# When a convolution block squares its input tiles: four early in order, four later, instead of eight in pairs

## The chip, the cores and the metric

The kernel runs on one core of a Trainium2 chip. The core has five engines that run their own instruction lists in order: TensorE (PE in the profile; PEld is its weight load), VectorE (DVE), ScalarE (ACT), GpSimd (POOL) and SyncE (SP). They meet only at semaphores, and each transfer (DMA) raises one when it has landed. The metric is the device time of one execution in microseconds (us); before the change it is 2095.65 us (median of three runs, 2095.22 to 2095.98).

## The reference

The program is a two-layer trunk on x of 1024 positions by 1024 channels, all in float32. Cut to the part that matters here, layer 0 starts so:

```python
def rms_norm(x, g):
    y = xf * lax.rsqrt(jnp.mean(xf * xf, axis=-1, keepdims=True) + EPS)
    return y * g

def short_conv_mixer(h, w_in, conv_k, w_out):
    b, c, u = jnp.split(h @ w_in, 3, axis=-1)
    y = causal_depthwise_conv(c * u, conv_k)      # width 3
    return (b * y) @ w_out

x = x + short_conv_mixer(rms_norm(x, mix_norm[0]), ...)   # layer 0
x = x + swiglu(rms_norm(x, ffn_norm[0]), ...)
# layer 1: dilated attention and a second swiglu, then a last rms_norm
```

The norm's scale per position needs the sum over all 1024 channels of the squares of x.

## The kernel before

**Tiles.** x is held transposed, as eight tiles X[0] to X[7] of 128 channels by 1024 positions. The gain is multiplied into the operands at once; the factor per position (`rstd`) is applied to the products' results, so that TensorE can start before the squares are summed.

**The products.** The projection by `conv_w_in` is done by Strassen's scheme in Winograd's form: twelve units u, each of seven products m. One product is twelve matmuls (`Strassen.mm`, L586 to L588): for each of four tiles k the high half of the weights with the high and the low half of the operand, then the low half of the weights with the high half of the operand. High and low halves carry a float32 number in two pieces. The first products, counted from 0, are (u,m) = (0,1) (1,1) (0,2) (1,2) (2,1) (2,2) (3,1) (3,2) (4,1) (4,2) (0,6) (1,6) (0,7) (1,7) (0,5) (1,5) (0,4) (1,4) (2,6) (0,3).

**What feeds them.** `load_raw` (L171, SP) loads a slab of weights, `raw`, of 512 KB. `combo` (L208, DVE) adds or subtracts such slabs. `split` makes the two halves `w` of the weights: ACT the high one (L147), DVE the low one (L148). The operand tiles `b` of the left side come from X by `operand` (L896 on ACT, L897 on DVE), or from sums `t2`, `t3` of X tiles by `hi` (L578 on ACT, L579 on DVE). `save` (L592, ACT) and `add` (L596, DVE) take results out of the PSUM banks.

**What sets the order.** Nothing is scheduled: instructions stand on each engine as the Python text issues them. `Conv.mix` has a function `start(n)` that runs before the matmuls of product n+1 are issued, that is, after product n. It makes operands (`next(prep)`), makes weights ahead (`ensure`), and calls `squares`. `mm` itself makes the weights two products ahead (three from n = 20 on), and when the next key needs a `combo`, that is made before.

**The squares.** `squares(n)` squares X[n] on ACT over all 1024 columns. X[0] and X[4] are squared straight into two sums, `norm.acc` and `self.upper` (L907). The other six go to a page `sq` (L910), and POOL issues a DMA of 512 KB that adds the page to its sum (L911). Two additions into the same sum may not be in flight at once, so the second waits until the first has landed; additions into the two sums may overlap. After product 18 DVE adds `upper` to `acc` (L1112).

**Pages.** Tiles of 128 by 1024 float32 come from one pool of 41 pages. A page is given out again when its last reader is known; whoever writes it next waits for that reader. A `sq` page is read by its adding DMA, so the next writer of that page waits until this DMA has landed.

Of the kernel before, what the change touches and what calls it, by code (L numbers as in the profile page):

```python
# [103 lines left out]
def trunk(ctx: ExitStack, tc: tile.TileContext, x, gains_in, cwi, ck, cwo, wqkv, wo, relb,  # L104
# [73 lines left out]
    def ensure(upto):  # L178
        while op_state[0] < min(upto + 1, len(ops)):
            key = ops[op_state[0] + 1][0] if op_state[0] + 1 < len(ops) else None  # L180
            if key in sums_of:
                sums_of.pop(key)()
            made[op_state[0]] = ops[op_state[0]][1]()
            op_state[0] += 1
# [208 lines left out]
    def run(*gens):  # L393
        for _ in zip(*gens):
            pass
        for g in gens:
            for _ in g:
                pass
# [485 lines left out]
    class Conv(Strassen):  # L884
# [182 lines left out]
        def mix(self, group1):  # L1067
            norm = self.norm
            prep = self.operands()
            stats = norm.stats(0, S)  # L1070

            def start(n):
                if n == 0:
                    next(prep)
                    ensure(self.at(2, 2))
                elif n in (1, 2):
                    next(prep)
                elif n == 3:
                    self.first(0)
                    ensure(self.at(4, 1))  # L1080
                    self.squares(0, 4)
                elif n == 4:
                    self.first(1)
                    ensure(self.at(4, 2))
                    self.squares(1)
                elif n == 5:
                    ensure(self.at(0, 6))
                    self.squares(5)
                elif n == 6:
                    ensure(self.at(1, 6))  # L1090
                    self.squares(2)
                elif n == 7:
                    next(prep)
                    self.squares(6, 3)
                elif n == 8:
                    self.first(2)
                    ensure(self.at(0, 7))
                    self.squares(7)
                elif n == 9:
                    next(prep)  # L1100
                    next(prep)
                elif n in (10, 12):
                    next(prep)
                elif n == 11:
                    next(prep)
                    self.first(3)
                elif n == 13:
                    self.first(4)
                elif n == 14:
                    next(prep, None)  # L1110
                elif n == 18:
                    nc.vector.tensor_tensor(out=norm.acc, in0=norm.acc, in1=self.upper, op=ALU.add)  # L1112
                    del self.upper
                elif n == 20:
                    self.ahead = 3

            def gather():
                next(stats)
                next(stats)

            def spread():
                run(stats)
                nc.scalar.activation(norm.acc, norm.rstd, AF.Square)
                self.ready = True

            self.base = op_state[1]
            ensure(self.at(0, 1))
            next(prep)
            ensure(self.at(0, 2))
            self.run(start, {(0, 3): gather, (2, 5): spread})  # L1130
            group1("co", self.plain, self.hid)

# [937 lines left out]
```

## Time and profile before

| what | value |
|---|---|
| median of three runs | 2095.65 us |
| lowest, highest | 2095.22, 2095.98 us |
| the profiled execution, its own time | 2097.12 us |
| its span in the profile | 2095.3 us |
| PE busy | 2077.0 us, 99% |
| DVE busy | 1756.8 us, 84% |
| ACT busy | 1023.0 us, 49% |
| POOL busy | 246.7 us, 12% |
| granted TensorE clock over the span | 0.998 |

In rows of the timeline stand the start, the duration, engine, line, operation, output and input, the count, and in brackets the idle time of the engine ahead of it with what ended it. Several equal instructions in a row are merged into one row (x4); its duration is then from the first start to the last end. DMA rows of SP and POOL are the issue of a transfer; it lands some us later. In rows of stretches (A:B) stand the length, busy time and count per engine, the granted TensorE clock, the busy share of the 16 DMA engines and the GB/s.

### The profile page before, as it was taken

What the parts mean: (1) busy time and instruction counts of PE and PEld (TensorE: products, weight loads), DVE (VectorE), ACT (ScalarE), POOL (GpSimd) and SP (SyncE); (2) the same over time, 40 slices, a digit from 0 to 9 for tenths busy, and PEclk for the clock granted to TensorE, in tenths of its full rate; (3) what the DMA queues carried; (4) which work ended last, traced back from release to release, by engine and by line L of the source; (5) the groups of instructions that cost most, each with busy time, mean ns of one, the idle gap of its engine ahead of it and who ended that gap; (6) DMA issues with size and microseconds to landing.
All of it is one profiled execution on the core that took longest, in us unless ns stands there. A gap on an engine that the chain in (4) does not pass through costs nothing.

```text
span 2095.3 us, 30793 instructions
## 1 busy us (share of the span) xinstructions
PE 2077.0 (99%) x10978; PEld 1790.3 (85%) x10978; DVE 1756.8 (84%) x3308; ACT 1023.0 (49%) x1892; POOL 246.7 (12%) x352
## 2 busy tenths in 40 slices
PE   9999999999999999999999999999999999999998
PEld 7788888888888888888789999998788888888887
DVE  8798759988888888968985888987998888888886
ACT  8333427444443455446544666665544434456433
POOL 1000000110100010010223333311011001001000
PEclk9999999999999999999999999999999999999999
DMA  7322643233333467451656867855223333359432
GB/s 221 96 96 71 227 135 81 101 106 109 103 106 103 139 209 214 130 169 61 228 194 196 214 166 228 235 185 146 71 90 107 106 101 112 109 196 246 159 96 81
DMA packets 124729, 300.72 MB, mean 144 GB/s; under 512 B 15084, under 2 KB 37694, under 8 KB 124576
## 3 DMA queue, kind: packets, MB, share of 16 engines
q1 hardware_dynamic: 90720, 201.94, 32.0%
q0 software_dynamic: 26224, 82.11, 12.6%
q10 hardware_dynamic: 7632, 14.70, 1.9%
q8 instruction: 87, 1.43, 0.3%
q14 instruction: 66, 0.54, 0.1%
HBM read 208.42 MB, written 82.93 MB: 139 GB/s over the span
## 4 chain that ended last, share of the span: by engine, by line
PE 91%; DVE 4%; ACT 1%; issue 1%; DMA 0%; DVEq 0%; SPq 0%; ACTq 0%
PE bank L588 20%; PE bank L586 20%; PE bank L587 20%; PE bank L1667 5%; PE bank L390 4%; PE bank L388 4%; PE bank L389 4%; PE bank L681 3%; PE bank L680 3%; PE bank L678 3%; PE bank L1536 2%; PE bank L1538 1%; PE bank L1537 1%; PE bank L1593 1%; PE bank L1592 1%; DVE b L579 1%
## 5 line engine op out<-in xcount | busy, mean ns | idle before, releaser
L588 PE MATMUL bank<-b,w 128*128 128x512 f32 x2008 | 782.9, 390 | 4.1 <-DVE w L148 3.9
L586 PE MATMUL bank<-b,w 128*128 128x512 f32 x2008 | 782.9, 390 | 3.1 <-ACT w L147 1.6
L587 PE MATMUL bank<-b,w 128*128 128x512 f32 x2008 | 782.6, 390 | 0.6 <-DVE b L897 0.6
L588 PEld LDWEIGHTS bank<-b,w 128*128 128x128 f32 x2008 | 377.4, 188 | 85.9 <-DVE w L148 7.6
L586 PEld LDWEIGHTS bank<-b,w 128*128 128x128 f32 x2008 | 377.6, 188 | 81.1 <-ACT w L147 3.5
L587 PEld LDWEIGHTS bank<-b,w 128*128 128x128 f32 x2008 | 377.6, 188 | 77.8 <-DVE b L897 1.4
L147 ACT ACTIVATE w<-combo 128x512 fp32r<-128x512 f32 (+2 forms) x496 | 254.2, 542 | 238.8 <-DVE combo L208 221.9
L148 DVE TENSOR_TENSOR w<-combo,w 128x512 fp32r<-128x512 f32 (+2 forms) x496 | 281.8, 581 | 40.6 <-ACT w L147 39.9
L592 ACT ACTIVATE part<-bank 128x512 f32<-128x512 f32 x192 | 114.4, 596 | 394.9 <-PE bank L588 392.4
L148 DVE TENSOR_TENSOR w<-raw,w 128x512 fp32r<-128x512 f32 (+2 forms) x348 | 192.5, 574 | 34.1 <-ACT w L147 34.1
L596 DVE TENSOR_TENSOR part<-part,bank 128x256 f32<-128x256 f32 (+1 forms) x372 | 174.8, 498 | 35.8 <-PE bank L588 18.8
L147 ACT ACTIVATE w<-raw 128x512 fp32r<-128x512 f32 (+2 forms) x348 | 170.7, 532 | 46.2 <-PE bank L588 12.2
L388 PE MATMUL bank<-w_hi,w 128*128 128x512 f32 (+1 forms) x400 | 151.3, 378 | 0.1
L390 PE MATMUL bank<-w_hi,w 128*128 128x512 f32 (+1 forms) x400 | 149.3, 373 | 0.7 <-DVE w L148 0.7
L389 PE MATMUL bank<-w_lo,w 128*128 128x512 f32 (+1 forms) x400 | 149.1, 373 | 0.0
L816 DVE TENSOR_TENSOR x<-x,bank 128x512 f32<-128x512 f32 x136 | 92.5, 680 | 28.0 <-PE bank L588 28.0
L208 DVE TENSOR_TENSOR combo<-raw 128x512 f32<-128x512 f32 (+1 forms) x176 | 113.8, 647 | 0.0
L507 DVE TENSOR_TENSOR x<-x,bank 128x512 f32<-128x512 f32 (+1 forms) x104 | 66.6, 643 | 54.0 <-PE bank L390 52.9
L390 PEld LDWEIGHTS bank<-w_hi,w 128*128 128x128 f32 x400 | 75.3, 188 | 15.0 <-DVE w L148 1.6
L388 PEld LDWEIGHTS bank<-w_hi,w 128*128 128x128 f32 x400 | 75.5, 189 | 12.0 <-ACT w L147 0.5
L389 PEld LDWEIGHTS bank<-w_lo,w 128*128 128x128 f32 x400 | 75.5, 189 | 11.6
L579 DVE TENSOR_TENSOR b<-hin,b 128x512 fp32r<-128x512 f32 x126 | 79.5, 684 | 6.0 <-ACT b L578 6.0
(228 smaller groups left out, 3342.1 us busy)
## 6 DMA issues: line engine op xcount, KB each, us to landing
hin<-part SPq DMA_DIRECT2D x126, 256.0 KB, 4.5
raw<-in_ffn_w_gate SPq DMA_DIRECT2D x44, 512.0 KB
raw<-in_ffn_w_up SPq DMA_DIRECT2D x44, 512.0 KB, 3.8
part<-sum POOLq DMA_DIRECT2D x72, 256.0 KB, 2.3
raw<-in_ffn_w_down SPq DMA_DIRECT2D x48, 384.0 KB, 3.7
raw<-in_attn_w_qkv SPq DMA_DIRECT2D x27, 512.0 KB, 3.7
raw<-in_conv_w_in SPq DMA_DIRECT2D x24, 512.0 KB, 3.6
part<-part POOLq DMA_DIRECT2D x36, 256.0 KB, 2.5
```

The lines of the kernel that those rows point to most:

```text
L147: nc.scalar.activation(hi, src, AF.Copy)
L148: low = lambda: eng.tensor_tensor(out=lo, in0=src, in1=hi, op=ALU.subtract)
L208: eng.tensor_tensor(out=c, in0=a, in1=b, op=op)
L388: nc.tensor.matmul(b, whi[:, a], ahi[:, s], start=first, stop=False)
L389: nc.tensor.matmul(b, whi[:, a], alo[:, s], start=False, stop=False)
L390: nc.tensor.matmul(b, wlo[:, a], ahi[:, s], start=False, stop=last)
L586: nc.tensor.matmul(b, hi[:, a], bhi, start=start and k == 0, stop=False, skip_group_check=True)
L587: nc.tensor.matmul(b, hi[:, a], blo, start=False, stop=False, skip_group_check=True)
L588: nc.tensor.matmul(b, lo[:, a], bhi, start=False, stop=k == n - 1, skip_group_check=True)
L592: nc.scalar.activation(t, b, AF.Copy)
L596: nc.vector.tensor_tensor(out=t, in0=t, in1=b, op=ALU.add)
L1667: nc.tensor.matmul(view(acc[ih], off, dims), vx[:, u * 192 + 128 * a:u * 192 + 128 * a + 128], rhs, start=first, stop=last)
```

## The change

`squares` is called with one tile at a time and at other places: X[0], X[1], X[2], X[3] after products 3, 4, 5, 6, and X[4], X[5], X[6], X[7] after products 9, 10, 11, 12. Before it was X[0] and X[4] after product 3, X[1] after 4, X[5] after 5, X[2] after 6, X[6] and X[3] after 7, X[7] after 8. The call also moves from the end of `start(n)` to its beginning, ahead of `next(prep)`, `first` and `ensure`. `squares` itself is the same.

```diff
             stats = norm.stats(0, S)
+            early = {3: 0, 4: 1, 5: 2, 6: 3, 9: 4, 10: 5, 11: 6, 12: 7}
 
             def start(n):
+                if n in early:
+                    self.squares(early[n])
                 if n == 0:
...
                 elif n == 3:
                     self.first(0)
                     ensure(self.at(4, 1))
-                    self.squares(0, 4)
                 elif n == 4:
                     self.first(1)
                     ensure(self.at(4, 2))
-                    self.squares(1)
                 elif n == 5:
                     ensure(self.at(0, 6))
-                    self.squares(5)
                 elif n == 6:
                     ensure(self.at(1, 6))
-                    self.squares(2)
                 elif n == 7:
                     next(prep)
-                    self.squares(6, 3)
                 elif n == 8:
                     self.first(2)
                     ensure(self.at(0, 7))
-                    self.squares(7)
```

Past the first 110 us or so of the span, the two programs differ only in which page a tile lies in. Names in the lists that follow: `x_99` to `x_106` are X[0] to X[7], `acc` and `acc2` the two sums, DMASW1 to DMASW6 the semaphores of the adding DMAs in their order, DMAHW those of SP's loads.

The adding DMAs on POOL, before:

```order
L911 DMA acc_374<-sq_402 128x1024 [waits Activation_49]
L911 DMA acc2_376<-sq_425 128x1024 [waits Activation_49]
L911 DMA acc_374<-sq_448 128x1024 [waits DMASW1_49,Activation_49]
L911 DMA acc2_376<-sq_476 128x1024 [waits DMASW2_49,Activation_49]
L911 DMA acc_374<-sq_479 128x1024 [waits DMASW3_49,Activation_49]
L911 DMA acc2_376<-sq_503 128x1024 [waits DMASW4_49,Activation_49]
```

and after the change:

```order
L911 DMA acc_364<-sq_393 128x1024 [waits Activation_49]
L911 DMA acc_364<-sq_417 128x1024 [waits DMASW1_49,Activation_49]
L911 DMA acc_364<-sq_442 128x1024 [waits DMASW2_49,Activation_49]
L911 DMA acc2_366<-sq_534 128x1024 [waits DMAHW7_49,DVE_49,Activation_49]
L911 DMA acc2_366<-sq_560 128x1024 [waits DMASW4_49,Activation_49]
L911 DMA acc2_366<-sq_585 128x1024 [waits DMASW5_49,Activation_49]
```

Before, the additions alternated between the sums and each waited for the one before the last; now three go into one sum and three into the other, and each waits for the one just ahead of it (the fourth, the first into the other sum, for its square alone).

ScalarE where product 6 gets its weights and the squares begin, before:

```order
L578 ACTIVATE b_347<-t2_313 128x512 [waits DVE_49]
L147 ACTIVATE w_365<-raw_111 128x512 [waits DMAHW7_49]
L147 ACTIVATE w_368<-raw_111 128x512
L147 ACTIVATE w_371<-raw_112 128x512 [waits DMAHW1_49]
L907 ACTIVATE acc_374<-x_99 128x1024
L907 ACTIVATE acc2_376<-x_103 128x1024 [waits DMAHW0_49]
L592 ACTIVATE part_392<-bank_379 128x512 [waits PE_49]
```

and after:

```order
L578 ACTIVATE b_347<-t2_313 128x512 [waits DVE_49]
L907 ACTIVATE acc_364<-x_99 128x1024
L147 ACTIVATE w_369<-raw_111 128x512 [waits DMAHW7_49]
L147 ACTIVATE w_372<-raw_111 128x512
L147 ACTIVATE w_375<-raw_112 128x512 [waits DMAHW1_49]
L592 ACTIVATE part_391<-bank_378 128x512 [waits PE_49]
```

The square of X[0] now stands ahead of the three weight halves, and that of X[4] has left this place.

ScalarE where the operands of m = 3 are made (`b_637` to `b_646`), ahead of the weights of product 17, before:

```order
L147 ACTIVATE w_621<-raw_108 128x512 [waits DMAHW0_49,Activation_49]
L896 ACTIVATE b_637<-x_103,gains_68 128x512 [waits Activation_49]
L896 ACTIVATE b_640<-x_104,gains_68 128x512
L896 ACTIVATE b_643<-x_105,gains_68 128x512 [waits Activation_49]
L896 ACTIVATE b_646<-x_106,gains_68 128x512 [waits DVE_49,PE_49]
L147 ACTIVATE w_656<-raw_113 128x512 [waits DMAHW2_49,DVE_49,PE_49]
```

and after:

```order
L147 ACTIVATE w_621<-raw_108 128x512 [waits DMAHW0_49]
L896 ACTIVATE b_637<-x_103,gains_68 128x512 [waits Activation_49]
L896 ACTIVATE b_640<-x_104,gains_68 128x512 [waits DMASW5_49,Activation_49]
L896 ACTIVATE b_643<-x_105,gains_68 128x512 [waits DVE_49,PE_49]
L896 ACTIVATE b_646<-x_106,gains_68 128x512 [waits DMASW6_49,Activation_49]
L147 ACTIVATE w_656<-raw_113 128x512 [waits DMAHW2_49,DVE_49,PE_49]
```

The second and the fourth of these operands now go to the pages of the squares of X[6] and X[7], and so wait for the fifth and the sixth adding DMA. On SP the first load after the start (`raw_619`) waited for the sixth adding DMA before and waits for the fourth now.

## The prediction

> **What bounds the kernel now.** I read the page first, then TensorE's waits up to 260 us, then the timelines of the engines there.
>
> ```profile
> span 2095.3 us, 30793 instructions
> PE 2077.0 (99%) x10978; PEld 1790.3 (85%) x10978; DVE 1756.8 (84%) x3308; ACT 1023.0 (49%) x1892; POOL 246.7 (12%) x352
> PE bank L588 <- DVE w L148: 2.7, 2, 2.0
> PE bank L586 <- ACT w L147: 1.6, 1, 1.6
> ```
>
> TensorE bounds the kernel, and the change touches no matmul. Only TensorE's idle time can move, and it can move only where the squares stand, in the first 65 us. Two stalls lie there: 1.6 us before product 6, for the high half of its weights, and 2.0 us inside product 17, for a low half.
>
> ```profile
> 25.13 0.50 PE L586 MATMUL bank<-b,w 128*128 128x512 f32 x1 [1.58 <-ACT w L147]
> 26.54 0.50 PE L588 MATMUL bank<-b,w 128*128 128x512 f32 x1 [0.67 <-DVE w L148]
> 57.02 0.39 PE L587 MATMUL bank<-b,w 128*128 128x512 f32 x1
> 59.43 0.80 PE L588 MATMUL bank<-b,w 128*128 128x512 f32 x1 [2.03 <-DVE w L148]
> 23.55:25.13 1.58, 0.00 (x0) 0.00 (x1) 1.48 (x3) 1.20 (x3) 0.00 (x0) 1.00 0.04 13
> 57.40:59.43 2.03, 0.00 (x1) 0.00 (x0) 1.35 (x3) 0.56 (x1) 0.00 (x0) 1.00 0.38 147
> 59.43:62.94 3.51, 3.51 (x9) 2.80 (x9) 3.51 (x7) 1.33 (x3) 0.00 (x0) 0.51 0.52 149
> 62.94:66.45 3.51, 3.51 (x17) 2.91 (x16) 1.78 (x3) 0.13 (x1) 0.00 (x0) 1.00 0.00 0
> ```
>
> The second stall costs more than its length: the granted clock was 0.51 in the 3.5 us behind it, and 9 matmuls started there against 17 in the next equal stretch. At half clock that is about 1.6 us lost. The first stall, 1.58 us, was followed by no lower clock, so 2.03 us is not far over what the gate lets pass.
>
> Why product 17 waits stands on VectorE.
>
> ```profile
> 52.13 0.68 DVE L148 TENSOR_TENSOR w<-raw,w 128x512 fp32r<-128x512 f32 x1
> 53.33 2.73 DVE L897 SCALAR_TENSOR_TENSOR b<-x,gains,b 128x512 fp32r<-128x512 f32 x4
> 55.98 0.68 DVE L208 TENSOR_TENSOR combo<-raw 128x512 f32<-128x512 f32 x1
> 58.08 0.69 DVE L208 TENSOR_TENSOR combo<-combo,raw 128x512 f32<-128x512 f32 x1 [1.42 <-DMA raw<-in_conv_w_in]
> 58.69 0.68 DVE L148 TENSOR_TENSOR w<-raw,w 128x512 fp32r<-128x512 f32 x1
> ```
>
> Its low half (58.69, done 59.37) stands behind four operands (L897) and two combinations of weights; the second of these waited for a slab. The slabs on SP:
>
> ```profile
> SPq L171 <- DMA acc<-sq: 32.2, 1, 32.2
> 49.07 0.33 SPq L171 DMA_DIRECT2D raw<-in_conv_w_in  x1
> 52.84 0.33 SPq L171 DMA_DIRECT2D raw<-in_conv_w_in  x1
> 54.76 0.33 SPq L171 DMA_DIRECT2D raw<-in_conv_w_in  x1
> ```
>
> SP sat 32 us on the last adding DMA before the first of these. The late slab is the second one; its issue at 52.84 follows the low half at 52.13, which frees its page (52.13 + 0.68 = 52.81), not the first slab.
>
> **The change, part by part.**
>
> *Product 6.* The square of X[0] now stands ahead of the three weight halves.
>
> ```profile
> 24.46 1.65 ACT L147 ACTIVATE w<-raw 128x512 fp32r<-128x512 f32 x3
> 25.80 1.89 DVE L148 TENSOR_TENSOR w<-raw,w 128x512 fp32r<-128x512 f32 x3
> 28.92 1.05 ACT L910 ACTIVATE sq<-x 128x1024 f32<-128x1024 f32 x1
> ```
>
> A square holds ScalarE for about 0.95 us (1.05, less the overlap with the next). The first weight half moves from 24.46 to 25.41, is ready at 26.04, and TensorE starts product 6 near 26.1. The low half can start at 26.1 instead of 25.80, so the third matmul moves only from 26.54 to about 26.85. TensorE is 0.3 us late from there. That lateness costs nothing, since it is idle at 57.40 anyway and what ends that wait is not in this chain: 0.
>
> *ScalarE from 26 to 50 us.* The eight squares are the same work. VectorE gets to the in-place subtraction about 1.2 us sooner, since four squares no longer stand ahead of the operands that it needs, and gives this back when the square of X[5] holds up the operands behind it. I put the low half of 52.13 at 51.9, and with it the second slab's issue at 52.6: a gain of 0.2 us at most if nothing else changes.
>
> *The chain of adding DMAs.* This is the term that counts.
>
> ```profile
> 30.28 0.88 POOL L911 DMA_DIRECT2D acc<-sq  x1 [28.30 <-ACT sq L910]
> 35.35 0.85 POOL L911 DMA_DIRECT2D acc<-sq  x1 [2.75 <-ACT b L578]
> 41.01 0.58 ACT L592 ACTIVATE part<-bank 128x512 f32<-128x512 f32 x1
> 43.83 0.86 POOL L911 DMA_DIRECT2D acc<-sq  x1 [1.98 <-ACT part L592]
> DMA to landing us min/median/max: 4.5/5.1/5.9
> ```
>
> The third DMA (35.35) waited for the first (30.28) to land: 5.07 us from issue to issue, 4.5 of it to landing. With two sums there were two under way, and POOL issued six from 30.28 to 43.83, one every 2.7 us. With one sum at a time each link takes 5.07. The square of X[1] runs 1.45 us sooner than at 28.92, since X[4]'s square (0.95) and a weight half (0.5) no longer stand ahead of it; so X[1], X[2], X[3] go out near 28.8, 33.9, 38.9 and disturb nobody. The square of X[5] stands on ScalarE behind the eviction that ran at 41.01; that one waits for product 10, whose end lets it run near 40.3, so the square is done near 41.9 and its DMA goes out at 42.2 (the 0.3 us of 28.92 + 1.05 to 30.28). It lands near 46.7. SP's first slab now waits for this one and goes out at 46.9, 2.2 us sooner than 49.07. Then X[6] goes out at 47.25 and X[7] only when X[6] has landed.
>
> These last two run beside slabs. Adding DMAs of the same size (512 KB) beside slabs are seen much later, in the down products of the feed-forward parts (`x` += `spill`, L831, groups of four). The landing of the first of each group, each from an answer of its own:
>
> ```profile
> DMA to landing us min/median/max: 5.6/5.6/5.6
> ...
> DMA to landing us min/median/max: 7.1/7.1/7.1
> ...
> DMA to landing us min/median/max: 7.4/7.4/7.4
> ...
> DMA to landing us min/median/max: 6.0/6.0/6.0
> ```
>
> With one slab ahead of it X[6] takes the least of these, 5.6: it lands at 52.9. X[7] goes out at 53.4, beside the slabs issued near 52.6 and 54.5; I take 6.1, so it lands at 59.5. Bounds: bare links (4.5 each) give 56.8; 5.9, the slowest of the first row, and then 7.1 give 60.8.
>
> *Who waits for X[7].* Its page goes to the last of the four operands of m = 3.
>
> ```profile
> 51.42 0.72 ACT L896 ACTIVATE b<-x,gains 128x512 fp32r<-128x512 f32 x1
> 54.27 0.63 ACT L147 ACTIVATE w<-raw 128x512 fp32r<-128x512 f32 x1 [2.12 <-PE bank L588]
> ```
>
> Nobody needs that operand before product 19. But ScalarE, which came to it at 51.42 and comes near 52.3 now, stops there, with the high half of product 17 (54.27) behind it; VectorE stops at the same operand (the fourth of 53.33), with both combinations and the low half behind it. From the landing: L896 0.7, L897 0.7, two combinations 0.7 and 0.6, the low half 0.7, 0.1 to TensorE: 3.5 us. Product 17 resumes at 59.5 + 3.5 = 63.0 instead of 59.43: +3.6 (bounds +0.9 and +4.9). The wait hides only if X[7] lands before 55.9. TensorE, VectorE and ScalarE move by the same amount behind it, so nothing is won back. The addition of the two sums (L1112) and the statistics stand behind products 18 and 19 and move along.
>
> *The clock.* The stall is now surely long enough for the lower clock. In the profiled execution it was paid already; that execution took 2097.12, 1.47 above the median, about what the lower clock costs. I take it that some executions did not pay it before, and that all do now: +0.8, half of 1.6. Bounds: -0.8, if half the slow stretch falls into the stall itself, and +1.7, if a second one follows.
>
> *Sum.* Against the profiled execution, which had paid the lower clock, 2097.12 + 3.6 = 2100.7. Against the median, 2095.65 + 3.6 + 0.8 = 2100.05. I forecast 2100.1.
>
> *A rule against it.* "DMA: Bandwidth & Descriptors" of the Trainium skill (section "Anatomy of one DMA — SWDGE (gpsimd) path") gives a DMA from GpSimd 2.0 us and its bytes over 436 GB/s: an estimate of 3.2 us for 512 KB. By it X[7] would land at 52.9 and the sum would be 0. The trace's 4.5 us, without a neighbour, disagrees, and the measurement decides.
>
> **The rivals.**
>
> *The wait on X[7] does not bind* (not slower). From 42.2 the chain has 13.7 us until 55.9; that needs links of 4.2 us, landing and reissue. The rule above would give it. Then the second slab alone sets product 17, at 59.2 (-0.2): 2095.4. If that slab also comes without its delay, VectorE's 1.42 us of waiting and the lower clock go too: 2095.65 - 1.4 - 1.6 = 2092.7, still within 0.2%. Against it: no DMA of line 911 landed under 4.5.
>
> *Bare links.* The slabs are through before the adding DMAs begin, and X[7] lands at 56.8: +0.9, and +0.3 for the clock: 2096.9. Against it: all four rows beside slabs are over 5.5.
>
> *The start decides.* The 0.95 us ahead of product 6 grows the first stall from 1.58 to 2.5 us, more than what brought the lower clock at 59.43. A slow stretch at 25 us would cost up to 1.6 us, but it would end in the idle time of product 17, like the 0.3 us above; 2100.1 stays.
>
> **How the numbers follow.** 0.2%, about what a measurement of this kernel can tell from no change, is 4.2 us: up to 2099.8. The wait on X[7] beside slabs has 0.85; its spread (landing 58.0 to 60.8, clock -0.8 to +1.7) gives 2097.5 to 2102.2, of which I put 0.57 above the bound and 0.28 below. Bare links have 0.08, the unbinding wait 0.07, nearly all within the bound (0.02 for a gain over 4.2 us that no row explains). So slower 0.57, same 0.28 + 0.08 + 0.05 = 0.41, faster 0.02. The range from 2096.9 to 2102.2 leaves the unbinding wait and the tails out.
>
> **What would show it.** In the profile after: ScalarE idle near 53 to 59 us in front of an L896, ended by the DMA of acc2; VectorE idle in front of its fourth L897; POOL's last three DMAs more than 5 us apart, the last issued after 53; SP's first slab near 47; TensorE idle first for a high half (L147), then for a low half (L148), together near 6 us between 56.5 and 63, and a clock near 0.5 behind. Wrong if the last adding DMA lands before 56, if TensorE resumes by 60, or if a stall appears outside the first 70 us.

## The result

The changed kernel takes 2103.19 us (median of 6 runs, 2102.71 to 2104.65), the kernel before beside it 2095.43 us (2094.52 to 2096.23, 6 runs). The ratio is 1.0037, with an interval from 1.0027 to 1.0048: 7.8 us slower. The forecast was 2100.1 with a range from 2096.9 to 2102.2, so the sign was right and the size was too small. The profiled execution took 2103.45 us.

The page after:

```profile
span 2101.7 us, 30794 instructions
PE 2079.5 (99%) x10978; PEld 1792.1 (85%) x10978; DVE 1757.8 (84%) x3308; ACT 1023.9 (49%) x1892; POOL 246.7 (12%) x352
```

What TensorE waits for in the first 260 us (us in total, times, the longest):

```profile
PE bank L586 <- ACT w L147: 7.8, 2, 5.3
PE bank L588 <- DVE w L148: 1.0, 1, 1.0
```

The work is the same. The waits for a high half (L147) have grown from 1.6 us to 7.8 us; one of the two is 5.3 us long. TensorE's timeline shows where:

```profile
26.05 0.50 PE L586 MATMUL bank<-b,w 128*128 128x512 f32 x1 [2.56 <-ACT w L147]
63.55 0.79 PE L586 MATMUL bank<-b,w 128*128 128x512 f32 x1 [5.26 <-ACT w L147]
65.75 0.79 PE L588 MATMUL bank<-b,w 128*128 128x512 f32 x1 [0.98 <-DVE w L148]
```

Product 6 starts at 26.05, 0.92 us later than before. Product 17 waits 5.26 us for its first high half and 0.98 us for the low half, and is through at 65.75, where it was at 59.43. These 6.32 us are nearly the whole difference of the two profiled executions (2103.45 - 2097.12 = 6.33). The rest of the 7.8 us is that the execution profiled before was a dear one, 1.69 us above the median of 2095.43, and the one profiled after only 0.26 above its own.

ScalarE and VectorE in front of product 17, after:

```profile
55.20 1.34 ACT L896 ACTIVATE b<-x,gains 128x512 fp32r<-128x512 f32 x2 [2.07 <-DMA acc<-sq]
62.26 0.72 ACT L896 ACTIVATE b<-x,gains 128x512 fp32r<-128x512 f32 x1 [5.72 <-DMA acc<-sq]
62.89 0.61 ACT L147 ACTIVATE w<-raw 128x512 fp32r<-128x512 f32 x1
63.02 0.75 DVE L897 SCALAR_TENSOR_TENSOR b<-x,gains,b 128x512 fp32r<-128x512 f32 x1 [5.64 <-ACT b L896]
63.68 0.69 DVE L208 TENSOR_TENSOR combo<-raw 128x512 f32<-128x512 f32 x1
65.02 0.68 DVE L148 TENSOR_TENSOR w<-raw,w 128x512 fp32r<-128x512 f32 x1
```

ScalarE stands 5.72 us in front of the last operand (X[7]'s) until an adding DMA lands. The high half of product 17 stands right behind that operand (62.89); VectorE stands 5.64 us in front of the same operand, with two combinations and the low half (65.02) behind it. Nothing but the landing of the sixth adding DMA holds them. The chain of adding DMAs on POOL's timeline (start of the issue; in brackets POOL's idle time):

```profile
28.78 0.88 POOL L911 DMA_DIRECT2D acc<-sq  x1 [26.80 <-ACT sq L910]
33.82 0.86 POOL L911 DMA_DIRECT2D acc<-sq  x1 [4.16 <-ACT b L578]
38.84 0.85 POOL L911 DMA_DIRECT2D acc<-sq  x1 [4.16 <-ACT acc L907]
43.71 0.85 POOL L911 DMA_DIRECT2D acc<-sq  x1 [4.01 <-ACT sq L910]
49.05 0.85 POOL L911 DMA_DIRECT2D acc<-sq  x1 [4.49 <-ACT sq L910]
55.64 0.85 POOL L911 DMA_DIRECT2D acc<-sq  x1 [5.74 <-DMA acc<-sq]
```

From issue to landing for the fourth, the fifth and the sixth, each an answer of its own on line 911:

```profile
DMA to landing us min/median/max: 4.8/4.8/4.8
...
DMA to landing us min/median/max: 6.1/6.1/6.1
...
DMA to landing us min/median/max: 6.5/6.5/6.5
```

The sixth lands near 62.2. The first three links are 5.0 us as forecast; the fourth DMA goes out at 43.71 instead of 42.2, and the links behind it are longer than forecast. Why the fourth was late stands two steps ahead of it on ScalarE:

```profile
41.87 0.60 ACT L592 ACTIVATE part<-bank 128x512 f32<-128x512 f32 x1 [1.57 <-PE bank L588]
42.36 1.05 ACT L910 ACTIVATE sq<-x 128x1024 f32<-128x1024 f32 x1
```

The eviction of product 10 waited for TensorE, and X[5]'s square stands behind it. TensorE was late because of its clock. The stretches of 3.41 us around the stalls, after (busy time and count by engine, then the granted clock, the DMA share and the GB/s):

```profile
24.27:27.68 3.41, 1.63 (x6) 1.07 (x7) 3.14 (x6) 3.41 (x7) 0.00 (x0) 1.00 0.00 0
27.68:31.09 3.41, 3.41 (x10) 2.63 (x9) 3.34 (x6) 3.23 (x5) 0.88 (x1) 0.50 0.31 60
58.40:61.81 3.41, 0.00 (x0) 0.00 (x0) 0.00 (x0) 0.00 (x0) 0.00 (x0) 1.00 1.00 233
61.81:65.22 3.41, 1.22 (x2) 0.50 (x2) 2.17 (x4) 1.27 (x3) 0.00 (x0) 0.50 0.04 14
65.22:68.63 3.41, 2.88 (x7) 2.30 (x8) 3.41 (x7) 1.66 (x3) 0.00 (x0) 0.50 0.52 143
```

The clock was halved for 3.41 us at 27.68, where 10 matmuls started, and for two such stretches from 61.81. Part of the latter lies in the stall itself and costs nothing. Behind the resumption at 65.75 lie 2.9 us of it, against 3.4 us before.

### The profile page after: what moved, and what is told of

It reads as the page before. It is cut to its first block, busy times and chain, and to the rows that moved or that the text cites. A ratio compares the mean times of both kernels' runs of the same rounds, so it can differ in the third digit from the quotient of the medians.

```text
span 2101.7 us, 30794 instructions
## 1 busy us (share of the span) xinstructions
PE 2079.5 (99%) x10978; PEld 1792.1 (85%) x10978; DVE 1757.8 (84%) x3308; ACT 1023.9 (49%) x1892; POOL 246.7 (12%) x352
## 4 chain that ended last, share of the span: by engine, by line
PE 92%; DVE 4%; DMA 2%; ACT 1%; issue 1%; SPq 0%; DVEq 0%; ACTq 0%; POOLq 0%
PE bank L588 20%; PE bank L586 20%; PE bank L587 20%; PE bank L1664 5%; PE bank L390 4%; PE bank L388 4%; PE bank L389 4%; PE bank L681 3%; PE bank L680 3%; PE bank L678 3%; PE bank L1533 2%; PE bank L1535 1%; PE bank L1534 1%; PE bank L1590 1%; PE bank L1589 1%; DVE b L579 1%
## 5 line engine op out<-in xcount | busy, mean ns | idle before, releaser
L588 PE MATMUL bank<-b,w 128*128 128x512 f32 x2008 | 783.4, 390 | 2.3 <-DVE w L148 2.2
L586 PEld LDWEIGHTS bank<-b,w 128*128 128x128 f32 x2008 | 378.2, 188 | 87.4 <-ACT w L147 10.2
L588 PEld LDWEIGHTS bank<-b,w 128*128 128x128 f32 x2008 | 377.9, 188 | 83.9 <-DVE w L148 5.5
L147 ACT ACTIVATE w<-combo 128x512 fp32r<-128x512 f32 (+2 forms) x496 | 254.2, 542 | 236.4 <-DVE combo L208 219.5
L148 DVE TENSOR_TENSOR w<-combo,w 128x512 fp32r<-128x512 f32 (+2 forms) x496 | 283.7, 586 | 39.8 <-ACT w L147 39.0
L592 ACT ACTIVATE part<-bank 128x512 f32<-128x512 f32 x192 | 114.5, 596 | 397.1 <-PE bank L588 394.6
L148 DVE TENSOR_TENSOR w<-raw,w 128x512 fp32r<-128x512 f32 (+2 forms) x348 | 193.7, 578 | 34.3 <-ACT w L147 34.3
L147 ACT ACTIVATE w<-raw 128x512 fp32r<-128x512 f32 (+2 forms) x348 | 170.7, 531 | 43.9 <-PE bank L681 10.5
L208 DVE TENSOR_TENSOR combo<-raw 128x512 f32<-128x512 f32 (+1 forms) x176 | 114.5, 651 | 0.0
```

Source lines behind the costliest of these rows:

```text
L147: nc.scalar.activation(hi, src, AF.Copy)
L148: low = lambda: eng.tensor_tensor(out=lo, in0=src, in1=hi, op=ALU.subtract)
L208: eng.tensor_tensor(out=c, in0=a, in1=b, op=op)
L586: nc.tensor.matmul(b, hi[:, a], bhi, start=start and k == 0, stop=False, skip_group_check=True)
L588: nc.tensor.matmul(b, lo[:, a], bhi, start=False, stop=k == n - 1, skip_group_check=True)
L592: nc.scalar.activation(t, b, AF.Copy)
```

## The experiments

Theory after the result: all of the loss is the chain of adding DMAs that ends at the page of X[7]'s square, plus clock. Rivals: the start of product 6 costs something by itself; the squares cost something by standing later; the clock costs nothing beyond what the kernel before paid. "Before" is the kernel before on the same chip, 21 to 27 runs in each set (medians 2095.50 for the first four, 2095.71 for the next four, 2095.32 for the last). Each set ran on another chip, so times from two sets, and the changed kernel's 2103.19, compare to a few tenths of a us only.

| label | kernel | median us | ratio to before, interval |
|---|---|---|---|
| e1_start_alone | before, X[0]'s square ahead of product 6's weights | 2095.51 | 0.9999 (0.9990 to 1.0008) |
| e2_start_back | changed, X[0]'s square back behind them | 2103.39 | 1.0036 (1.0023 to 1.0049) |
| e3_sums_alternate | changed, additions alternate between the sums | 2097.36 | 1.0009 (1.0000 to 1.0018) |
| e4_page_held | changed, X[7]'s operand gets another page | 2097.72 | 1.0013 (1.0004 to 1.0022) |
| e5_filled_17 | changed, zeros in front of product 17 | 2102.09 | 1.0030 (1.0019 to 1.0042) |
| e6_filled_both | changed, zeros in front of 6 and 17 | 2100.73 | 1.0025 (1.0016 to 1.0034) |
| e7_before_filled | before, zeros in front of 6 and 17 | 2094.63 | 0.9994 (0.9985 to 1.0003) |
| e8_weights_first | before, product 17's weights made first | 2094.25 | 0.9993 (0.9984 to 1.0002) |
| e9_traffic_twice | e6, two slabs copied to DRAM besides | 2104.96 | 1.0042 (1.0030 to 1.0055) |
| e10_alternate_filled | e3 with zeros | 2095.22 | 0.9998 (0.9989 to 1.0007) |
| e11_weights_and_6 | e8 with zeros in front of 6 | 2092.97 | 0.9988 (0.9979 to 0.9997) |
| e12_filled_again | e6, one execution more | 2100.62 | |

### Does the start cost anything

The first part of the change alone, on the kernel before:

```diff
                 elif n == 3:
+                    self.squares(0)
                     self.first(0)
                     ensure(self.at(4, 1))
-                    self.squares(0, 4)
+                    self.squares(4)
```

> The kernel before, with one edit: the square of X[0] goes ahead of the weights of product 6, all other squares and their adding DMAs stay. Theory (the start costs only through what waits for TensorE later): the first stall grows from 1.6 to about 2.6 us and a slow clock stretch may follow it, but the adding DMAs here hang on no eviction, so TensorE's lateness of up to 1.9 us ends in the idle time of product 17, which shrinks to below 1 us and brings no second slow stretch: 2094 to 2096.5 us, the kernel before within 1.5. Rival (the start is paid in full wherever it stands): 0.95 + 1.6 us more, 2098.

It takes 2095.51 us, as before; the interval leaves room for about 2 us either way. TensorE's timeline:

```profile
26.32 0.50 PE L586 MATMUL bank<-b,w 128*128 128x512 f32 x1 [1.42 <-ACT w L147]
```

The stall did not grow to 2.6 us here, but only because TensorE came late itself: the last matmul ahead of the stall starts at 24.51, where it was at 23.16, since between 7.10 and 10.51 us TensorE started 9 matmuls, against 16 in the next 3.41 us. Product 6 still starts 1.19 us later than before (26.32 against 25.13). The adding DMAs go out only 0.24 us later (30.52 to 44.07 against 30.28 to 43.83), and product 17's low half is taken at 59.42, where it was at 59.43: in the kernel before, a late product 6 ends in the idle time of product 17. The same from the other side, in the changed kernel (the first call only gives the three pages out in the same order):

```diff
-                if n in early:
+                if n == 3:
+                    self.squares()
+                elif n in early:
                     self.squares(early[n])
...
                     ensure(self.at(4, 1))
+                    self.squares(0)
```

> The changed kernel, with the square of X[0] put back behind the weights of product 6; pages and all adding DMAs as changed. Theory (two causes: the chain of adding DMAs that holds the operand of X[7], and the start, which made the square of X[5] 1.5 us late): no slow stretch at 28 us, the square of X[5] near 40.8, X[7] lands near 60.6 instead of 62.2, product 17 resumes near 64.2 instead of 65.75: 2100 to 2102, some 1.5 to 3 under the changed kernel and 5 to 6 over the one before. Rival (the start with its slow clock is the whole loss): back to 2095.4. Rival (the start costs nothing): 2103.2.

It takes 2103.39 us: nothing came back, and the range of this run's theory, 2100 to 2102, is missed. Still the fourth adding DMA is late here too, at 43.12, and the clock was halved behind product 6, though the stalls there are as before the change (1.57 and 0.67 us). TensorE's timeline, the second of the two stalls:

```profile
26.18 0.60 PE L588 MATMUL bank<-b,w 128*128 128x512 f32 x1 [0.67 <-DVE w L148]
```

And the stretches there, by engine, with the clock after the counts:

```profile
23.04:26.45 3.41, 1.17 (x4) 0.57 (x4) 3.31 (x6) 2.88 (x5) 0.00 (x0) 1.00 0.03 12
26.45:29.86 3.41, 3.41 (x9) 2.63 (x9) 3.38 (x7) 3.41 (x6) 0.88 (x1) 0.50 0.01 2
```

So it is not the position of X[0]'s square that brings the half clock at product 6. The stall there can bring it with either order. What differs is who hears of it.

### The two ends of the chain

First the seriality is taken away. Additions alternate between the sums, as in the kernel before; the times of the squares stay those of the change:

```diff
-                acc = self.upper if n > 3 else norm.acc
-                if n % 4 == 0:
+                acc = self.upper if n % 2 else norm.acc
+                if n < 2:
```

> The changed kernel, with squares added to the two sums in turn (even tiles into one, odd tiles into the other), at the changed places. Theory (the chain is the loss, because three DMAs in a row go into one sum): X[6] no longer waits for X[5], X[7] waits for X[5] alone and lands near 55.5 to 57 instead of 62.2; product 17 resumes near 59.5 to 60.5: 2095 to 2097.5. Rival (the place of the squares or the slabs beside them are the loss, not the one sum): 2101 to 2103.

2097.36 us: 5.8 of the 7.8 us are gone. The last adding DMA goes out at 48.59 instead of 55.64. TensorE does not wait for a high half at product 17 any more, only 2.3 us for the low one, as it did before. The timeline:

```profile
48.59 0.85 POOL L911 DMA_DIRECT2D acc<-sq  x1 [1.47 <-ACT sq L910]
60.82 0.50 PE L588 MATMUL bank<-b,w 128*128 128x512 f32 x1 [2.30 <-DVE w L148]
```

Then the chain is left alone and only the wait at its end is taken away: one column of the page of X[7]'s square is read once more after product 18, so that the operand of X[7] is given another page.

```diff
                     nc.gpsimd.dma_start(out=acc, in_=sq, accum_op=ALU.add)
+                    self.last_sq = sq
...
                 elif n == 18:
                     nc.vector.tensor_tensor(out=norm.acc, in0=norm.acc, in1=self.upper, op=ALU.add)
-                    del self.upper
+                    nc.vector.tensor_copy(scratch, self.last_sq[:, :1])
+                    del self.upper, self.last_sq
```

> The changed kernel, with the page of X[7]'s square read once more after product 18 (one column copied on VectorE), so that the operand of X[7] gets another page; the chain of adding DMAs stays as it is. Theory (the DMA hurts only because an operand waits for its page): the sixth adding DMA still lands near 61 to 62, but ScalarE no longer stops for it; VectorE still waits for the fifth (near 55) and for the second slab; product 17 resumes near 60 to 61.5: 2096 to 2098. Rival (late DMAs hold the slabs or the engines whatever page is used): 2101 to 2103.

2097.72 us, so 5.5 us are gone. The sixth adding DMA goes out at 54.37 and takes 6.7 us, so it lands near 61.0. But the last three operands are made from 53.92 to 55.87, behind the fifth, and product 17 resumes at 60.00. Its timeline on POOL, ScalarE and TensorE:

```profile
54.37 0.85 POOL L911 DMA_DIRECT2D acc<-sq  x1 [5.76 <-DMA acc<-sq]
53.92 1.95 ACT L896 ACTIVATE b<-x,gains 128x512 fp32r<-128x512 f32 x3 [2.10 <-DMA acc<-sq]
60.00 0.80 PE L588 MATMUL bank<-b,w 128*128 128x512 f32 x1 [2.57 <-DVE w L148]
```

And from the sixth's issue to its landing:

```profile
DMA to landing us min/median/max: 6.7/6.7/6.7
```

The late sum by itself costs nothing; the page is what makes it dear. Either end of the mechanism gives back the same 5.5 to 5.8 us, and both leave about 2 us over before.

### The clock

Products of a weight tile of zeros keep TensorE at work while it waits; they add zero to the bank. In front of product 17 there are 24:

```diff
+FILLER = {(1, 4): 24}
...
+            for i in range(FILLER.get((u, m), 0) if self.key == CONV else 0):
+                nc.tensor.matmul(d["p"], scope["zeros"], self.b[m][0][0], start=m == 1 and i == 0, stop=False,
+                                 skip_group_check=True)
```

> The changed kernel, with 24 products of a weight tile of zeros in front of product 17, in its own bank, so that TensorE has something to do while product 17's weights are late; the result is the same. Theory (part of the 7.8 us lost is TensorE running at half clock after its long stall at 58 to 66 us, 6.8 us of such a stretch in the profiled execution): no half clock behind 64 us, and 2100.0 to 2101.8. Rival (the loss is the late weights alone, the chain of adding DMAs and the page of X[7]'s square): 2102.5 to 2103.8, as the changed kernel.

2102.09 us lies between the two expectations, 1.1 us under the changed kernel, and 0.3 us short of the theory's. The zeros ended before the weights came, and in the profiled execution, the slowest of the six, the half clock had not gone but moved behind the wait for the low half, as two stretches there show:

```profile
63.31:66.72 3.41, 1.36 (x5) 0.84 (x6) 3.33 (x6) 1.16 (x3) 0.00 (x0) 1.00 0.00 0
66.72:70.13 3.41, 3.41 (x10) 2.67 (x9) 3.41 (x6) 1.26 (x2) 0.00 (x0) 0.50 0.55 154
```

With 10 more in front of product 6 (`FILLER = {(3, 1): 10, (1, 4): 24}`):

> As the kernel before it, with 10 such products of zeros in front of product 6 too, whose stall of 2.6 us was followed by half clock in the profiled execution, on which the eviction before X[5]'s square stood. Theory (the half clock at 28 us made X[5]'s square, and so the chain of adding DMAs, 1 to 1.5 us late): X[5]'s square ends near 41 us, the last adding DMA goes out near 54 us instead of 55.6, and the time is 2098.5 to 2100.5. Rival (the start costs nothing, as where X[0]'s square went back behind the weights): the same time as with product 17 filled alone, within 0.4 us.

2100.73 us: 1.4 us less again, and 2.5 us less than the changed kernel, a little short of the theory's range. The rival of this run, that the start costs nothing, is out: filling product 6 gave more than filling product 17, and eight of these ten executions are faster than all six with zeros in front of product 17 alone. In the profile there is no half clock between 5 us and the last 5 us of the span; the same stretch at 27.68 now holds 17 matmuls instead of 10, and the fourth adding DMA goes out at 42.09, which was the forecast's 42.2. (The kernel with the page held, where no half clock followed product 6 in the profile, has it at 42.40 without any zeros.)

```profile
27.68:31.09 3.41, 3.41 (x17) 2.83 (x16) 3.34 (x6) 3.41 (x6) 0.88 (x1) 1.00 0.31 60
```

Its timeline (lines stand up to four further down in this kernel, so L915 is L911, L900 is L896 and L589 is L588):

```profile
42.09 0.85 POOL L915 DMA_DIRECT2D acc<-sq  x1 [2.35 <-ACT sq L914]
60.72 0.72 ACT L900 ACTIVATE b<-x,gains 128x512 fp32r<-128x512 f32 x1 [5.79 <-DMA acc<-sq]
64.22 0.50 PE L589 MATMUL bank<-b,w 128*128 128x512 f32 x1 [1.46 <-DVE w L149]
```

The kernel before, filled in the same way (`FILLER = {(3, 1): 7, (1, 4): 8}`):

> The kernel before, with 7 products of zeros in front of product 6 and 8 in front of product 17, where it waits 1.6 and 2.0 us. If the kernel before pays for half clock behind these waits in most executions, it becomes 1.0 to 2.0 us faster (2093.5 to 2094.5); if it does not, nothing changes (2095.2 to 2095.8), and then the changed kernel's clock loss is all new.

2094.63 us, 1.1 us under the before of its set and 0.1 us short of the first expectation; the interval (0.9985 to 1.0003) does not quite leave out no change. The granted clock speaks for it in part: it is 0.999 over the span in all 11 runs, while the before of that set has 0.998 in 16 of 27 runs, and one stretch of 3.41 us at half clock takes 0.0008 from that mean. But the 11 runs of before with 0.999 have a median of 2095.48, only 0.4 us under the 16 others (2095.85) and still 0.85 above the filled kernel. So the zeros give about 1 us at the median, and how much of that is half clock is not shown.

What was left in the kernel with alternating sums, filled too (10 and 10):

> The changed kernel with the additions alternating between the two sums (2097.4 us), and products of zeros in front of products 6 (10) and 17 (10). Theory (all that is left of the loss there is half clock behind the two stalls, and the later squares cost nothing by themselves): 2094.2 to 2095.2, as the kernel before with such products (2094.6). Rival (the later squares cost something beside the chain and the clock): 2096 to 2097.4.

2095.22 us, at the upper edge of the theory's range and 0.8 us from the rival's. The zeros give the alternating kernel 2.1 us, and 0.6 are left over the filled kernel before, which the intervals do not tell from nothing. Its 11 runs without zeros sort by the granted clock: the three with 0.999 have a median of 2094.65, the four with 0.998 of 2097.24, the four with 0.997 of 2098.93. The later places of the squares cost nothing that can be measured; the rest goes with the clock.

### The links beside slabs

Two slabs are copied to DRAM right behind their load, in the kernel filled at both places, so that twice the traffic moves beside X[6]'s adding DMA:

```diff
+TWICE = (7, 8)
...
             nc.sync.dma_start(raw_tile[i][:, :raw_src[i].shape[1]], raw_src[i])
+            if i in TWICE:
+                nc.sync.dma_start(dram.tile([128, 1024], F32, name=f"copy{i}", tag=f"copy{i}", bufs=1), raw_src[i])
```

> The changed kernel with products of zeros in front of products 6 and 17 (2100.7 us), and behind the first and the second slab a copy of that slab to DRAM, 512 KB each, that nobody reads. Theory (the last two links are longer than 5.07 us because slabs move beside them): the link from X[6]'s to X[7]'s adding DMA, 6.6 us without the copies, becomes 7 to 8, that DMA goes out at 54.5 to 55.5 instead of 54.0, and the time is 2101.2 to 2103.5. Rival (the links are longer for another reason, such as what GpSimd does): 6.6 us again and 2100.2 to 2101.2.

2104.96 us, and more than the theory expected. X[6]'s adding DMA takes 9.3 us to land (6.1 without the copies), and the link is 9.85 us. POOL's timeline:

```profile
47.77 0.85 POOL L918 DMA_DIRECT2D acc<-sq  x1 [4.50 <-ACT sq L917]
57.62 0.85 POOL L918 DMA_DIRECT2D acc<-sq  x1 [9.00 <-DMA acc<-sq]
```

And from the issue of the first of these to its landing:

```profile
DMA to landing us min/median/max: 9.3/9.3/9.3
```

X[7]'s, with one slab beside it where there were two, lands after 5.5 us instead of 6.6. So the traffic beside them sets the last links: 4.5 to 4.8 us to landing with no slab, 6.1 with a slab, 9.3 with a slab and its copy, both 512 KB each, and the next pair behind. Of the 5.26 us between the two profiled executions (2104.96 - 2099.70) the chain has 2.45: product 17 gets its low half at 66.67 instead of 64.22. A stretch of half clock that came back behind this wait (67.05 to 70.46, granted clock 0.50) has about 1.7, and a wait of 1.1 us for a DMA in layer 1's attention, far from here, the rest. The first slabs wait for the chain (SP's first load goes out when the fourth adding DMA has landed), so the chain brings its own neighbours.

> A second look at the changed kernel with products of zeros in front of products 6 and 17 (median 2100.7, the first profiled execution 2099.7). If the two last links of the chain vary by themselves, they differ here from 5.35 and 6.60 us by some tenths, and the time of this execution with them; if not, they are the same within 0.1 us.

The second execution took 2100.62 us, 0.92 more than the first. The link between the fourth and the fifth is 5.35 us again, the one between the fifth and the sixth is 6.42 us, 0.18 less than in the first, and from the sixth's issue to landing it is 6.8 us (6.6 in the first): each of the last two varies by about 0.2 us, the two together by less. So the longer time is not theirs. Most of it, 0.78 us, was there before the chain began; the first adding DMA on POOL's timeline, in the first execution:

```profile
28.79 0.88 POOL L915 DMA_DIRECT2D acc<-sq  x1 [26.80 <-ACT sq L914]
```

and in the second:

```profile
29.57 0.88 POOL L915 DMA_DIRECT2D acc<-sq  x1 [27.59 <-ACT sq L914]
```

### A version that beats both

In the kernel before, product 17's low half stands behind two combinations that only product 18 and later ones read. Made in the other order:

```diff
+            late = ops[op_state[0]][0] == ("m", (CONV, 1), 4)
-            if key in sums_of:
+            if key in sums_of and not late:
                 sums_of.pop(key)()
             made[op_state[0]] = ops[op_state[0]][1]()
+            if key in sums_of:
+                sums_of.pop(key)()
             op_state[0] += 1
```

> The kernel before, with the two weight halves of product 17 split ahead of the sum of slabs that product 18 and later ones read. Theory (product 17's wait of 2.0 us in the kernel before is for work on VectorE that stands ahead of its weights): the wait falls to 0.5 us or less and product 18 waits at most 1 us: 2092.5 to 2094.5. Rival (the wait moves on to product 18 whole): 2095.0 to 2096.0.

2094.25 us, in the theory's range; product 17 does not wait at all. The interval still holds no change. With 7 products of zeros in front of product 6 besides:

> The kernel before with product 17's weights made first (2094.25 us), and 7 products of zeros in front of product 6. If half clock behind product 6's stall of 1.6 us still costs something there: 2093.0 to 2093.9. If not: 2094.0 to 2094.5.

2092.97 us, 0.03 under the first expectation, and the only kernel here whose interval (0.9979 to 0.9997) lies wholly under 1: 2.4 us under before, 10.2 under the changed kernel. On VectorE the low half (55.60) now stands ahead of the combinations, 3.1 us sooner than 58.69, and TensorE's one wait in front of a low half in the first 260 us is 0.7 us, at product 6. VectorE's timeline (in this kernel L149 and L212 are L148 and L208, and L592 is the matmul of L588):

```profile
55.60 0.68 DVE L149 TENSOR_TENSOR w<-raw,w 128x512 fp32r<-128x512 f32 x1
56.20 0.68 DVE L212 TENSOR_TENSOR combo<-raw 128x512 f32<-128x512 f32 x1
```

and TensorE's wait:

```profile
PE bank L592 <- DVE w L149: 0.7, 1, 0.7
```

## Where the prediction was right and where it was wrong

| step of the prediction | forecast | measured |
|---|---|---|
| product 6 starts | 26.1 | 26.05 |
| X[1], X[2], X[3] go out | 28.8, 33.9, 38.9 | 28.78, 33.82, 38.84 |
| X[5] goes out | 42.2 | 43.71 (42.09 at full clock) |
| SP's first slab | 46.9 | 48.68 (47.06 at full clock) |
| SP's second slab | 52.6 | 54.16 (52.54 at full clock) |
| X[5] to X[6], issue to issue | 5.05 | 5.34 |
| X[6] to X[7] | 6.15 | 6.59 |
| X[7] lands after | 6.1 | 6.5 |
| landing to resumption | 3.5 | 3.6 |
| product 17 resumes | 63.0 | 65.75 |
| clock, at the median | +0.8 | about +1.4 (estimate) |

The step that failed is the one on the start, which let a late product 6 end in product 17's idle time; two links of the chain and the clock were too small besides.

*Right.* The wait that the forecast named is the one that came: ScalarE in front of X[7]'s operand, the high half behind it, VectorE behind the same operand. The two kernels that cut the chain at one end each showed it. That it binds had been given 0.85, and the rivals "does not bind" and "bare links" are out: X[7] lands at 62.2, not before 55.9 or at 56.8.

*Wrong: "The chain of adding DMAs", two terms.* The resumption came 2.75 us later than 63.0. Of that, 1.5 is X[5]'s late start, 0.3, 0.45 and 0.4 are the three links from X[5] on, and 0.1 the way from the landing to TensorE. The forecast took for X[6] the least of four rows beside other slabs (5.6 to landing; it was 6.1) and for X[7] 6.1 (it was 6.5); the bound, 7.1, held it. For these two, the doubled traffic shows that what moves beside them makes them longer. X[5]'s landed after 4.8 us, against the forecast's 4.5, with no slab beside it; why, stays open. The Trainium skill's page "DMA: Bandwidth & Descriptors", section "Anatomy of one DMA — SWDGE (gpsimd) path", would have given 3.2 us by the estimate made above; the measured 4.8 to 6.5 us are still further from it than the 4.5 of before.

*Wrong: "The start decides".* The forecast saw that a slow stretch could follow product 6, and let it "end in the idle time of product 17, like the 0.3 us above". That asked only what TensorE does with its lateness. ScalarE's eviction of product 10 waits for TensorE, X[5]'s square stands behind that eviction, and the chain starts with that square: so 1.5 us of half clock at 28 us went through the chain to product 17, whose stall it lengthened instead of ending in it. Filling product 6 gave 1.4 us back. In the kernel before, where no square stands that late and two additions are under way at a time, a product 6 that was 1.19 us late cost nothing at product 17 (59.42 against 59.43, in the run with X[0]'s square moved alone).

*Wrong in size: "The clock".* +0.8 was forecast, half of one slow stretch. By the zeros, the changed kernel pays 2.5 us of clock (2103.19 - 2100.73), 1.4 of it at product 6, and the kernel before at most 1.1 (2095.71 - 2094.63): +1.4 as an estimate from medians, and the 1.4 at product 6 reaches product 17 through the chain. The reason given, that a stall of 1.58 us is let pass and one of 2.03 is not far over the limit, was no reason: see the last section.

*The sum at the median.* With the zeros, so with next to no half clock, the chain costs 2100.73 - 2094.63 = 6.1 us, where 3.6 was forecast; with the clock's 1.4 that is 7.5 of the 7.8 us. Of the missing 2.5 in the chain the profiles show 1.25 (5.35 + 6.60 + 6.6 against 5.05 + 6.15 + 6.1). The remaining 1.25 stays open: the filled kernel's executions spread from 2099.70 to 2103.12, both that were profiled lie in the lower half, and the two filled kernels' profiled executions are only 4.4 us apart (2099.70 - 2095.33). Executions differ elsewhere too: TensorE's wait for a DMA in layer 1's attention is between 0 and 1.1 us in the profiles here. One sum of the forecast does not come out: a landing at 58.0 and a clock of -0.8 give 2095.65 + 2.07 - 0.8 = 2096.9, not 2097.5; the range began at 2096.9 all the same.

## What to carry to other kernels

Before work is moved that adds into one place, write down the chain of its transfers with their landing times, and then look up whose page the last one holds: the price is set by what waits for that page in order, not by when the sum is needed. When a stall is booked as "ends in idle time", follow every engine that waits for the late one, not only the late one itself, since an eviction can start a chain. Transfers beside others are to be taken from rows with as much traffic beside them, and holding one page a little longer gave 5.5 us back here, nearly as much as splitting the chain (5.8).

## What the runs showed of the hardware

*The clock goes by stretches of 3.41 us, and by how much of one TensorE was busy.* Apart from the last 9 us of the spans, half clock came in stretches of 3.41, 6.83 and 10.24 us, one to three times the same length. Cut into such stretches, counted back from the first half one, an execution shows when the next is slow. The kernel before:

```profile
21.89:25.30 3.41, 1.83 (x9) 1.22 (x8) 3.28 (x6) 1.99 (x4) 0.00 (x0) 1.00 0.34 129
56.02:59.43 3.41, 1.38 (x7) 0.80 (x5) 1.99 (x5) 0.56 (x1) 0.00 (x0) 1.00 0.49 159
59.43:62.84 3.41, 3.41 (x8) 2.73 (x9) 3.41 (x6) 1.33 (x3) 0.00 (x0) 0.50 0.53 154
```

The changed kernel with the page held:

```profile
21.95:25.36 3.41, 1.95 (x9) 1.29 (x7) 3.28 (x6) 1.76 (x3) 0.00 (x0) 1.00 0.38 143
25.36:28.77 3.41, 2.39 (x9) 1.72 (x10) 3.23 (x7) 3.41 (x7) 0.00 (x0) 1.00 0.01 2
```

The stretches with 1.38 us of TensorE (above), 1.63, 1.17 and 1.36 (the changed kernel, the start put back, product 17 filled) were each followed by a slow one; those with 1.83, 1.95 and 2.39 were not. In these runs the limit lies between 1.63 and 1.83 us, near half a stretch. The page held had a stall of 2.48 us at 23.9 to 26.4, longer than the 2.03 us that brought the half clock before, and got away, because a border fell into it and shared it out. The position of the borders differs from one execution to the next (27.68, 26.45 and 25.36 are such borders near product 6 in three profiles), so a stall of about 2 us can be followed by half clock in one execution and not in another, and a mean over them has to be forecast. Two kinds of stretches read differently. Where the clock was halved already, 2.88 us of slow matmuls were followed by full clock, and 2.43 us (the start put back, from 64 us on) by another slow stretch. And in the first 10 us one stretch with 1.85 us (the alternating sums, filled) was followed by a slow one. The Trainium skill's page "TensorE: Matmul & The Clock Gate", section "What's actually happening", speaks of a window of 3413 ns that runs freely, and the stretches agree with it. The section "HAM oscillation — how this bites in real kernels" of the same page of the Trainium skill gives as a rule that no idle gap may be longer than about 3.4 us; that is too wide here, where gaps of 2.03 us and of 1.57 with 0.67 were enough.

*An adding DMA took a fifth to a half longer beside loads, and twice as long beside loads and their copies.* In these chains 512 KB took 4.5 to 4.8 us to land alone, 5.5 to 6.8 beside slabs and 9.3 beside slabs and copies.
